# A one-core hybrid layer on TensorE: side transfers pinned behind their sources, weight loads ahead of their splits, the preparation of heads spread out, centring copies pinned on ScalarE

## The chip, the cores and the metric

One core of a Trainium2 chip runs the whole kernel. The metric is the device time of one execution in microseconds (us); lower is better. The engines are TensorE (PE, with its weight loads PEld), VectorE (DVE), ScalarE (ACT), GpSimd (POOL) and SyncE (SP), which issues the DMAs here. Each engine works through its own instructions in order.

## The reference

One layer on a sequence of 256 frames of width 4096, batch 1, in float32. One input projection feeds two groups of heads and a gate; their gated outputs go through an output projection and a LayerNorm.

```python
x <- LayerNorm(ALPHA * x + W_out(concat(fox, rwkv) * silu(z)))
# input projection: [fox q|k|v|f, rwkv r|k|v|w_down|a_down, gate z]
# fox:  16 heads of 128: logit[t,s] = q_t.k_s/sqrt(Dh) + sum_{s<j<=t} log f_j, softmax over s<=t, times v
# rwkv: 32 heads of 64: RWKV-7 time mixing in chunks of 64 frames, with a 2-tap shift of its inputs,
#       low-rank decay and in-context rate, per-head GroupNorm and a bonus term (r.k * r_k) * v
```

In a chunk the recurrence becomes a triangular system, which is solved row by row; between chunks a state is carried on with matmuls.

## The kernel before, in words

**Weights.** The two projections stream their weights as tiles of 512 KB. A tile `w{n}_{b}_{q}` belongs to group n (0 to 7), block b (0 to 3) and piece q (0 to 15) of the depth; the output projection's tiles are `wo{b}_{q}`. SP loads a tile (tag `wr`, four buffers), ACT casts it to a high half `...h` (L140, four buffers), DVE subtracts to get a low half `...l` (L141, three buffers), and PE does twelve 128x512 matmuls with it: x-high by w-high (L146), x-low by w-high (L147), x-high by w-low (L148). The two instructions of L140 and L141 are called the split of a tile here. In the profile the digits in names are left out, so `w_12l` stands for the low half of piece 12 of any group and block; the order rows keep the block and piece.

**Side work.** Everything else runs beside this stream, as Python generators in a list `sides`. After every six matmuls the kernel calls `slot()`, which advances each of them to its next `yield`; `wait(n)` yields n times. For each group n (four rwkv heads as two pairs i, two fox heads) these are:

- `prepare(i)`: token shift, low-rank decay and rates, the running sum of decays (L416), exponentials, the key's norm `np` by matmul (L467, L468), its reciprocal `n2` (L470, L472), and the factors `lt`, `BK` and `sb` (L448 to L476).
- `rwkv(n)`: products of chunks `gp` on PE (L491), masked on DVE to `gb` and `lt` (L508, L516), stored as `nd` and loaded back as `Nb` (L511, L512); then the triangular system, a chain of 31 pairs TENSOR_TENSOR (L535) and TENSOR_REDUCE (L538) on DVE; after it the centring: mean `vm` (L563), `SV` (L570) and its copies `UV` on ACT (L573); then inverses and state matmuls (L579 to L647).
- In the course of the chain v is transposed (L542), stored and loaded back in another order (`turn`, `vv`), and multiplied into the bonus (`bon`, L549). The constant `V_AT` says at which row.
- `fox(i)`: logits, exponentials and read-out of an attention head; `gate` multiplies the result by the gate and splits it into `hl`, which goes to DRAM (`hd`, L365).
- `unload`: copies a finished block from PSUM to `bk` (ACT), transposes it on DVE (L750), stores it (`bt`, in `turn`), and loads it back as `raw`, `fq`, `fk`, `zf`, `zr`.

**What sets the order.** A scheduler takes the program and puts each engine's instructions in an order by dependences and its own estimates; a tile's buffers come free when their last reader is done. `tc.keep_in_program_order(x)` pins x: on its engine it comes behind everything that was traced before it. The first pair of a chain is pinned so, and the v transposes.

The weights reach the stream through `fetch()`, which issues a tile's load and its split together, up to three tiles ahead of the matmuls. The functions as they were:

Of the kernel before, what the change touches and what calls it, by code (L numbers as in the profile page):

```python
# [17 lines left out]
P = 128  # L18
# [23 lines left out]
LAG = 2  # L42
LAND = 3
BEHIND = 13
V_AT = 6
W = {"fo": 3, "vs": 2, "np": 6, "gp": 5, "tp": 4, "d1": 8, "d2": 12, "xp": 3, "fs": 4, "fp": 5}
NB = D // OB
# [37 lines left out]
def layer(ctx: ExitStack, tc: tile.TileContext, xt, xtok, w_lora, w_main, muv, w_o, up, par, mulora, fbias, lng, lnb, cst, out):  # L85
# [124 lines left out]
    rpool = None  # L210
    ready = []

    def fetch():
        if stream:
            name, src = stream.pop()
            raw = wpool.tile([P, 1024], F32, tag="wr", name=name, bufs=4)
            nc.sync.dma_start(out=raw, in_=src.rearrange("p k c -> p (k c)"))
# [12 lines left out]
    def weights(name):  # L230
        while len(ready) < 3 and stream:
            fetch()
        got, hi, lo = ready.pop(0)
        assert got == name
        return hi, lo
# [35 lines left out]

    def turn(src, cols, name):
        d = dram.tile([cols // B, B, 2, 4, B], F32, tag=f"dt{cols}", name=name, bufs=2)
# [69 lines left out]

    kept_h = set()
    ht = {}
    closed = []
# [9 lines left out]
    def gate(y, key, k):  # L356
        far = k < FAR
        h = rp.tile([P, S], F32, tag="h", name=f"h{k}")
        nc.vector.scalar_tensor_tensor(h, y, 0.5, szs[key], ALU.mult, ALU.mult)
        pool, tag, bufs = (rp, "hl", 2) if far else (xpool, f"x{k}", 1)  # L360
        hl = pool.tile([P, 2, S], F32R, tag=tag, name=f"hl{k}", bufs=bufs)
        nc.scalar.copy(hl[:, 0, :], h)
        nc.vector.tensor_tensor(hl[:, 1, :], h, hl[:, 0, :].bitcast(F32), ALU.subtract)
        if far:
            nc.sync.dma_start(out=hd[k], in_=flat(hl).bitcast(F32))  # L365
            kept_h.add(k)
        else:
            ht[k] = hl
# [62 lines left out]
    def prepare(i):  # L431
# [30 lines left out]
        for j in range(2):  # L462
            h = HALF[j]
            nc.vector.tensor_tensor(BK[h, :, KB[j][1]], ch(k)[h], ch(eI)[h], ALU.mult)
# [6 lines left out]
        nc.scalar.copy(q["bon"][:, u, :], nps[:, S:])  # L471
        nc.vector.reciprocal(n2, n2)  # L472
        nc.vector.scalar_tensor_tensor(ae, ae, 0.5, n2, ALU.mult, ALU.mult)
        for j in range(2):
            h = HALF[j]
            nc.vector.scalar_tensor_tensor(BK[h, :, KB[j][0]], ch(kr)[h], column("k_k", i)[h], ch(ae)[h], ALU.mult, ALU.mult)  # L476
        prepared.add(i)

    def rwkv(n):
# [41 lines left out]
        for u in range(2):  # L521
# [3 lines left out]
            nc.scalar.copy(flat(BKt[:, u]), tp)  # L525
        yield from wait(W["d1"])
        prod = rp.tile([P, 2, NJ, B], F32, tag="prod", name=f"prod{n}")
        xc = rp.tile([P, 2, NJ, B], F32, tag="xc", name=f"xc{n}")
# [4 lines left out]
        for t, s in enumerate(range(B - 2, -1, -1)):  # L533
# [4 lines left out]
            nc.vector.tensor_reduce(xc[:, :, :, s : s + 1], prod[:, :, :, s:], AX.X, ALU.add)  # L538
            if t == V_AT:
                vst = UV[0].rearrange("p u c v -> p (u c v)").rearrange("p (m q) -> p m q", m=2)  # L540
                for a in range(2):
                    tc.keep_in_program_order(nc.vector.transpose(vst[:, a, :], vs_[n][:, a, :]))  # L542
            if t == V_AT + 2:
                vdr = turn(vst, 2 * P, f"vt{n}")
            if t == V_AT + 4:
                vv[n] = rp.tile([P, 2, S], F32, tag="s2", name=f"vv{n}")
                nc.sync.dma_start(out=vv[n], in_=turned_back(vdr))
            if t == V_AT + 8:
                nc.vector.tensor_tensor(flat(bon), flat(bon), flat(vv[n]), ALU.mult)  # L549
                for u in range(2):  # L550
                    nc.scalar.activation(bon[:, u], bon[:, u], AF.Identity, bias=column("gn_bias", i0 + u))
                bonned.add(n)
            if t % ROWS == ROWS - 1:
# [11 lines left out]
        for j in range(2):  # L565
            o = HALF[1 - j]
            for c in range(2):
                h = HALF[c]
                for a in range(2):
                    nc.vector.scalar_tensor_tensor(  # L570
                        SV[j][o, :, 2 * a + c, :], vm[h, a, :, j].unsqueeze(2).to_broadcast([C, 2, HD]), -1.0 / HD, vt[h, a, :, j, :], ALU.mult, ALU.add
                    )
            nc.scalar.copy(UV[j][o], SV[j][o])  # L573
            nc.gpsimd.memset(SV[j][HALF[j], :, 0, :], 0.0)
# [89 lines left out]
        for u in range(2):  # L664
# [4 lines left out]
            while f"r{i0 + u}" not in szs or 2 * (i0 + u) + 1 >= FAR and not closed:  # L669
                yield  # L670
            gate(yc[:, u], f"r{i0 + u}", 2 * (i0 + u) + 1)
        done.add(n)
# [3 lines left out]
    def fox(i, q, k, vt):  # L676
# [32 lines left out]
        while f"f{i}" not in szs or 2 * i >= FAR and not closed:  # L709
            yield  # L710
        gate(o, f"f{i}", 2 * i)
        foxed.add(i)
# [24 lines left out]
    def unload(n, b, bk, vt):  # L737
# [10 lines left out]
        if not last:  # L748
            for m in range(2):
                nc.vector.transpose(bk[:, m, :], bk[:, m, :])  # L750
            yield
            d = turn(bk, OB, f"bt{n}_{b}")
            unloading.clear()
            yield
        if b == 0:
            for u in range(2):
                i = 2 * n + u
                while n and n - 1 not in bonned:
                    yield
                raw = rp.tile([P, 2, S], F32, tag="s2", name=f"raw{i}")  # L760
                nc.sync.dma_start(out=raw, in_=turned_back(d[8 * u : 8 * u + 8]))
# [19 lines left out]
        else:  # L781
            for j, t in enumerate((fq, fk, zf, zr)):
                nc.sync.dma_start(out=t, in_=d[4 * j : 4 * j + 4].rearrange("b i m a t -> (b i) (m a t)"))
                if j % 2:
# [269 lines left out]
```

## Time and profile before

| | |
|---|---|
| median of 3 runs | 1972.52 us (1970.55 to 1972.55) |
| the profiled execution | 1970.62 us; span from first to last instruction 1968.8 us |
| granted TensorE clock, mean | 0.996 |
| busy: PE, PEld, DVE, ACT, POOL | 99%, 81%, 70%, 50%, 4% |
| instructions on PE, DVE, ACT, POOL | 10169, 2212, 1485, 111 |
| DMA | 420.14 MB, mean 213 GB/s |

A row of a timeline shows start and duration in us, the engine, the line and operation, what is written from what, shapes, how often, and in brackets the idle time of the engine ahead of it and what ended that. A row of the waits shows the waiting engine and line, the releaser, the sum in us, how often, and the longest. SPq is SP's DMA queue. The profiled execution lies at the low end of the three times.

### The profile page before, as it was taken

What the parts mean: (1) busy time and instruction counts of PE and PEld (TensorE: products, weight loads), DVE (VectorE), ACT (ScalarE), POOL (GpSimd) and SP (SyncE); (2) the same over time, 40 slices, a digit from 0 to 9 for tenths busy, and PEclk for the clock granted to TensorE, in tenths of its full rate; (3) what the DMA queues carried; (4) which work ended last, traced back from release to release, by engine and by line L of the source; (5) the groups of instructions that cost most, each with busy time, mean ns of one, the idle gap of its engine ahead of it and who ended that gap; (6) DMA issues with size and microseconds to landing.
All of it is one profiled execution on the core that took longest, in us unless ns stands there. A gap on an engine that the chain in (4) does not pass through costs nothing.

```text
span 1968.8 us, 28251 instructions
## 1 busy us (share of the span) xinstructions
PE 1942.4 (99%) x10169; PEld 1587.5 (81%) x10169; DVE 1370.1 (70%) x2212; ACT 983.3 (50%) x1485; POOL 75.1 (4%) x111
## 2 busy tenths in 40 slices
PE   9999999999999999999999999999999999999998
PEld 8877787878787878787878787878787878888886
DVE  6588568866785778577857785778577857755555
ACT  6554465456545654564456445644564454444332
POOL 0010001000100010001000100010001000000000
PEclk9999999999999999999999999999999999999999
DMA  9567666867676767676767676767677777766664
GB/s 336 149 212 217 193 208 193 241 185 221 200 231 191 220 201 224 192 220 206 226 184 230 199 227 186 228 205 225 187 219 215 242 269 250 242 198 199 195 194 169
DMA packets 269393, 420.14 MB, mean 213 GB/s; under 512 B 142338, under 2 KB 171028, under 8 KB 269252
## 3 DMA queue, kind: packets, MB, share of 16 engines
q1 hardware_dynamic: 268820, 417.91, 69.4%
q8 instruction: 80, 1.31, 0.3%
q14 instruction: 61, 0.50, 0.1%
q10 hardware_dynamic: 432, 0.43, 0.1%
HBM read 388.61 MB, written 29.64 MB: 212 GB/s over the span
## 4 chain that ended last, share of the span: by engine, by line
PE 94%; DVE 3%; ACT 1%; issue 1%; DMA 1%; POOL 0%; SPq 0%; POOLq 0%; DVEq 0%; ACTq 0%
PE acc L146 23%; PE acc L148 23%; PE acc L147 22%; PE oacc L821 6%; PE oacc L822 6%; PE oacc L823 6%; PE yp L647 1%; PE gp L491 1%; PE up L622 1%; PE rh L595 1%; PE sp L631 0%; DVE w_12l L141 0%; ACT w_14h L140 0%; PE fsp L686 0%; PE tp L524 0%
## 5 line engine op out<-in xcount | busy, mean ns | idle before, releaser
L538 DVE TENSOR_REDUCE xc<-prod 128x8 f32<-128x16 f32 (+30 forms) x248 | 73.1, 295 | 6.3
L535 DVE TENSOR_TENSOR prod<-Nb,xc 128x8 f32<-128x8 f32 (+30 forms) x248 | 71.8, 290 | 7.0 <-DMA Nb<-nd 0.3
L141 DVE TENSOR_TENSOR w_8l<-w,w_8h 128x1024 fp32r<-128x1024 f32 x31 | 38.0, 1225 | 52.5 <-PE acc L148 27.3
L140 ACT CAST w_7h<-w 128x1024 fp32r<-128x1024 f32 x31 | 32.6, 1051 | 57.4 <-DMA w<-in_w_main_dram 43.0
L141 DVE TENSOR_TENSOR w_5l<-w,w_5h 128x1024 fp32r<-128x1024 f32 x31 | 40.3, 1300 | 29.9 <-PE acc L148 10.8
L148 PE MATMUL acc<-w_12l,x 128*128 128x512 f32 x124 | 47.7, 402 | 10.7 <-DVE w_12l L141 10.7
L141 DVE TENSOR_TENSOR w_6l<-w,w_6h 128x1024 fp32r<-128x1024 f32 x31 | 37.8, 1219 | 28.0 <-ACT UV L625 15.8
L141 DVE TENSOR_TENSOR w_3l<-w,w_3h 128x1024 fp32r<-128x1024 f32 x31 | 37.9, 1222 | 27.2 <-PE acc L148 26.1
L140 ACT CAST w_15h<-w 128x1024 fp32r<-128x1024 f32 x31 | 32.7, 1054 | 48.1 <-DMA w<-in_w_main_dram 25.7
L140 ACT CAST w_8h<-w 128x1024 fp32r<-128x1024 f32 x31 | 32.6, 1050 | 47.8 <-PE acc L147 30.4
L146 PE MATMUL acc<-w_6h,x 128*128 128x512 f32 x124 | 49.7, 401 | 4.8 <-ACT w_6h L140 4.8
L141 DVE TENSOR_TENSOR w_7l<-w,w_7h 128x1024 fp32r<-128x1024 f32 x31 | 37.8, 1219 | 22.5 <-PE acc L148 10.9
L140 ACT CAST w_14h<-w 128x1024 fp32r<-128x1024 f32 x31 | 32.6, 1052 | 39.9 <-PE acc L147 16.9
L141 DVE TENSOR_TENSOR w_9l<-w,w_9h 128x1024 fp32r<-128x1024 f32 x31 | 37.9, 1223 | 20.8 <-PE acc L148 10.5
L141 DVE TENSOR_TENSOR w_4l<-w,w_4h 128x1024 fp32r<-128x1024 f32 x31 | 37.9, 1221 | 20.8 <-PE acc L148 20.8
L146 PE MATMUL acc<-w_5h,x 128*128 128x512 f32 x124 | 50.7, 409 | 0.0
L146 PE MATMUL acc<-w_0h,x 128*128 128x512 f32 x124 | 50.6, 408 | 0.0
L146 PE MATMUL acc<-w_1h,x 128*128 128x512 f32 x124 | 50.5, 408 | 0.0
L146 PE MATMUL acc<-w_3h,x 128*128 128x512 f32 x124 | 50.4, 406 | 0.0
L146 PE MATMUL acc<-w_4h,x 128*128 128x512 f32 x124 | 50.0, 403 | 0.0
L146 PE MATMUL acc<-w_2h,x 128*128 128x512 f32 x124 | 49.9, 402 | 0.0
L146 PE MATMUL acc<-w_13h,x 128*128 128x512 f32 x124 | 49.8, 401 | 0.0
(812 smaller groups left out, 6486.6 us busy)
## 6 DMA issues: line engine op xcount, KB each, us to landing
w<-in_w_main_dram SPq DMA_DIRECT2D x496, 512.0 KB
wo<-in_w_o_dram SPq DMA_DIRECT2D x128, 512.0 KB
bt<-bk SPq DMA_DIRECT2D x88, 128.0 KB
Nb<-nd SPq DMA_DIRECT2D x16, 512.0 KB
wr<-in_w_main_dram SPq DMA_DIRECT2D x15, 512.0 KB
hd<-hl SPq DMA_DIRECT2D x29, 256.0 KB
h<-hd SPq DMA_DIRECT2D x29, 256.0 KB
raw<-bt SPq DMA_DIRECT2D x16, 256.0 KB
```

Source lines behind the costliest of these rows:

```text
L140: nc.scalar.copy(hi[:, :n], src[:, :n])
L141: nc.vector.tensor_tensor(lo[:, :n], src[:, :n], hi[:, :n].bitcast(F32), ALU.subtract)
L146: nc.tensor.matmul(acc[:, :n], xs[k][:, 0, tt], hi[:, o : o + n], start=(k == 0), stop=False)
L147: nc.tensor.matmul(acc[:, :n], xs[k][:, 1, tt], hi[:, o : o + n], start=False, stop=False)
L148: nc.tensor.matmul(acc[:, :n], xs[k][:, 0, tt], lo[:, o : o + n], start=False, stop=(k == KT - 1))
L491: nc.tensor.matmul(gp[u][j][:, c * P : (c + 1) * P], BK[h, u, c, :], lt[j][h, u, c, :], start=True, stop=True)
L535: first = nc.vector.tensor_tensor(prod[:, :, :, s + 1 :], nb[:, :, s : s + 1, s + 1 :].to_broadcast([P, 2, NJ, w]), xc[:, :, :, s + 1 :], ...
L538: nc.vector.tensor_reduce(xc[:, :, :, s : s + 1], prod[:, :, :, s:], AX.X, ALU.add)
L595: nc.tensor.matmul(rh[HALF[j], u * C : (u + 1) * C], lt[j][:, u, c, 0:C], SV[j][:, u, c, :], start=True, stop=True)
L821: nc.tensor.matmul(acc, ht[k][:, 0, tt], hi, start=(k == 0), stop=False)
L822: nc.tensor.matmul(acc, ht[k][:, 1, tt], hi, start=False, stop=False)
L823: nc.tensor.matmul(acc, ht[k][:, 0, tt], lo, start=False, stop=(k == KT - 1))
```

## The change

Five things change; the computation does not.

1. `issue()` pins a DMA on SP's queue. The stores of `turn`, the loads of `raw`, `fq`, `fk`, `zf`, `zr`, `vv` and the stores `hd` use it. `turn` is now a generator that yields after every two stores (or every one); `gate` is a generator that waits three slots (`SENT`) before its store and holds while more than one is on its way; `unload` waits two slots ahead of `turn`.
2. `load()` issues weight tiles up to three ahead of their splits; `fetch()` takes them from `raws`. The buffers stay four.
3. `prepare` has more `yield`s; the reciprocal of `n2` is pinned and two slots pass after it. `W["np"]` goes from 6 to 4.
4. The transposes of v, `turn`, `vv` and `bon` become a generator `turns()` that advances by one step with each row of the chain.
5. The `UV` copies of the centring are pinned on ACT.

```diff
-V_AT = 6
-W = {"fo": 3, "vs": 2, "np": 6, "gp": 5, "tp": 4, "d1": 8, "d2": 12, "xp": 3, "fs": 4, "fp": 5}
+SENT = 3
+W = {"fo": 3, "vs": 2, "np": 4, "gp": 5, "tp": 4, "d1": 8, "d2": 12, "xp": 3, "fs": 4, "fp": 5}
...
-    def fetch():
+    raws = []
+
+    def load():
         if stream:
             name, src = stream.pop()
             raw = wpool.tile([P, 1024], F32, tag="wr", name=name, bufs=4)
             nc.sync.dma_start(out=raw, in_=src.rearrange("p k c -> p (k c)"))
+            raws.append((name, raw))
+
+    def fetch():
+        while len(raws) < 3 and stream:
+            load()
+        if raws:
+            name, raw = raws.pop(0)
...
-    def turn(src, cols, name):
+    def issue(out, src):
+        tc.keep_in_program_order(nc.sync.dma_start(out=out, in_=src))
+
+    def turn(src, name, each=2):
...
         for a in range(4):
-            nc.sync.dma_start(out=d[:, :, :, a, :].rearrange("q i m t -> i m q t"), in_=s[B * a : B * (a + 1)])
+            issue(d[:, :, :, a, :].rearrange("q i m t -> i m q t"), s[B * a : B * (a + 1)])
+            if a % each == each - 1:
+                yield
         return d
...
     def gate(y, key, k):
         far = k < FAR
+        while len(storing) > 1:
+            yield
...
         if far:
-            nc.sync.dma_start(out=hd[k], in_=flat(hl).bitcast(F32))
+            storing.append(k)
+            yield from wait(SENT)
+            issue(hd[k], flat(hl).bitcast(F32))
             kept_h.add(k)
+            storing.remove(k)
...
         nc.vector.scalar_tensor_tensor(sb[:, 1, :], r, column("r_k", i), k, ALU.mult, ALU.mult)
+        yield
...
         nc.vector.tensor_tensor(sl, flat(sb), sh.bitcast(F32), ALU.subtract)
+        yield
...
         nc.scalar.copy(lt[1][HALF[1]], lt[0][HALF[1]])
+        yield
...
         nc.scalar.copy(q["bon"][:, u, :], nps[:, S:])
-        nc.vector.reciprocal(n2, n2)
+        yield
+        tc.keep_in_program_order(nc.vector.reciprocal(n2, n2))
+        yield from wait(2)
...
+        def turns():
+            yield from wait(4)
...
+                tc.keep_in_program_order(nc.vector.transpose(vst[:, a, :], vs_[n][:, a, :]))
+            yield from wait(3)
+            d = yield from turn(vst, f"vt{n}", 1)
+            yield from wait(2)
...
+            issue(vv[n], turned_back(d))
+            yield from wait(4)
+            nc.vector.tensor_tensor(flat(bon), flat(bon), flat(vv[n]), ALU.mult)
...
+        other = turns()
...
-            if t == V_AT:
...
-            if t == V_AT + 2:
...
-            if t == V_AT + 4:
...
-            if t == V_AT + 8:
...
+            next(other, None)
...
-            nc.scalar.copy(UV[j][o], SV[j][o])
+            tc.keep_in_program_order(nc.scalar.copy(UV[j][o], SV[j][o]))
...
-            yield
-            d = turn(bk, OB, f"bt{n}_{b}")
+            yield from wait(2)
+            d = yield from turn(bk, f"bt{n}_{b}")
```

What this does to the order, at three places. The first is DVE in group 1, block 1, between the splits of pieces 11 and 12, where the second head of a pair is prepared; names with `_2` and `_3` ahead of the number belong to heads 2 and 3 of the list. Before:

```order
L141 TENSOR_TENSOR w_1_11l<-w_1_11_3000,w_1_11h 128x1024
L472 RECIPROCAL n_2926<-n_2926 128x256
L414 TENSOR_SCALAR tw_2952<-tw_2952 128x256
L473 SCALAR_TENSOR_TENSOR ae_2681<-ae_2681,n_2926 128x256
L416 SCALAR_TENSOR_TENSOR L_2969<-cs,tw_2952 128x256
L476 SCALAR_TENSOR_TENSOR BK_2845<-s_2_2827,prm,ae_2681 64x4x64 x2
L448 TENSOR_TENSOR k_2986<-s_3_2884,am_2982 128x256
L426 SCALAR_TENSOR_TENSOR ae_2984<-ta_2954,eI_2974 128x256
L451 SCALAR_TENSOR_TENSOR sb_2988<-s_3_2881,prm,k_2986 128x256
```

After:

```order
L141 TENSOR_TENSOR w_1_11l<-w_1_11_2913,w_1_11h 128x1024
L493 TENSOR_SCALAR n_2966<-np_2963 128x256
L141 TENSOR_TENSOR w_1_12l<-w_1_12_2933,w_1_12h 128x1024
L496 RECIPROCAL n_2966<-n_2966 128x256
L141 TENSOR_TENSOR w_1_13l<-w_1_13_2951,w_1_13h 128x1024
L498 SCALAR_TENSOR_TENSOR ae_2793<-ae_2793,n_2966 128x256
L141 TENSOR_TENSOR w_1_14l<-w_1_14_2976,w_1_14h 128x1024
L501 SCALAR_TENSOR_TENSOR BK_2873<-s_2_2861,prm,ae_2793 64x4x64 x2
```

Before, thirteen instructions (these and `lt`, `lt` and `BK` twice) stood ahead of the split of piece 12; now one does, and the others stand between later splits. It is the same in the groups after it.

The second is DVE in group 0, block 3, at the end of the chain. Before:

```order
L538 TENSOR_REDUCE xc_1610<-prod_1609 128x8
L535 TENSOR_TENSOR prod_1609<-Nb_1465,xc_1610 128x8x31
L538 TENSOR_REDUCE xc_1610<-prod_1609 128x8
L563 TENSOR_REDUCE vm_2034<-vs_1339 128x8
L570 SCALAR_TENSOR_TENSOR SV_0_1484<-vm_2034,vs_1339 64x2x64 x4
L570 SCALAR_TENSOR_TENSOR SV_0_1485<-vm_2034,vs_1339 64x2x64 x4
L141 TENSOR_TENSOR w_3_6l<-w_3_6_1855,w_3_6h 128x1024
L141 TENSOR_TENSOR w_3_7l<-w_3_7_1893,w_3_7h 128x1024
```

After:

```order
L582 TENSOR_REDUCE xc_1692<-prod_1691 128x8
L579 TENSOR_TENSOR prod_1691<-Nb_1547,xc_1692 128x8x31
L582 TENSOR_REDUCE xc_1692<-prod_1691 128x8
L141 TENSOR_TENSOR w_3_7l<-w_3_7_1804,w_3_7h 128x1024
L722 SCALAR_TENSOR_TENSOR lg_1962<-fsp_1959,ct,nb_1903 128x128
```

The chain begins behind w_3_0l now (before: behind w_2_12l) and ends ahead of w_3_7l, with 27 of its instructions in one piece behind w_3_6l; `vm` and `SV` stand ahead of the split of `w_0_1` of the next group. In groups 1 to 6 the chain begins behind w_2_12l instead of w_2_10l, and ends ahead of w_3_7l in both.

The third is ACT at the same place. Before:

```order
L140 CAST w_3_5h<-w_3_5_1833 128x1024
L573 COPY UV_0_1486<-SV_0_1484 64x512
L573 COPY UV_0_1487<-SV_0_1485 64x512
L140 CAST w_3_6h<-w_3_6_1855 128x1024
L140 CAST w_3_7h<-w_3_7_1893 128x1024
```

After:

```order
L140 CAST w_0_1h<-w_0_1_2086 128x1024
L140 CAST w_0_2h<-w_0_2_2109 128x1024
L604 COPY UV_0_1568<-SV_0_1566 64x512
L604 COPY UV_0_1569<-SV_0_1567 64x512
L890 COPY bk_3_2171<-acc_3_0_1724 128x512
L890 COPY bk_3_2171<-acc_3_1_1725 128x512
L140 CAST w_0_3h<-w_0_3_2153 128x1024
```

The copies have moved from between the casts of block 3, pieces 5 and 6, to behind the cast of piece 2 of the next group's first block.

More of the change, by code (lines that the diff above doesn't have):

```diff
@@ L230, in weights @@
     def weights(name):
-        while len(ready) < 3 and stream:
+        while len(ready) < 3 and (stream or raws):
             fetch()
@@ L344, in layer @@
     kept_h = set()
+    storing = []
     ht = {}
@@ L476, in prepare @@
             nc.vector.scalar_tensor_tensor(BK[h, :, KB[j][0]], ch(kr)[h], column("k_k", i)[h], ch(ae)[h], ALU.mult, ALU.mult)
+        yield
         prepared.add(i)
@@ L670, in rwkv @@
                 yield
-            gate(yc[:, u], f"r{i0 + u}", 2 * (i0 + u) + 1)
+            yield from gate(yc[:, u], f"r{i0 + u}", 2 * (i0 + u) + 1)
         done.add(n)
@@ L710, in fox @@
             yield
-        gate(o, f"f{i}", 2 * i)
+        yield from gate(o, f"f{i}", 2 * i)
         foxed.add(i)
@@ L760, in unload @@
                 raw = rp.tile([P, 2, S], F32, tag="s2", name=f"raw{i}")
-                nc.sync.dma_start(out=raw, in_=turned_back(d[8 * u : 8 * u + 8]))
+                issue(raw, turned_back(d[8 * u : 8 * u + 8]))
                 yield from wait(LAND)
@@ L782, in unload @@
             for j, t in enumerate((fq, fk, zf, zr)):
-                nc.sync.dma_start(out=t, in_=d[4 * j : 4 * j + 4].rearrange("b i m a t -> (b i) (m a t)"))
+                issue(t, d[4 * j : 4 * j + 4].rearrange("b i m a t -> (b i) (m a t)"))
                 if j % 2:
```

19 lines of the change are left out of this document (8 added, 11 removed).

## The prediction

> **What bounds the kernel now.** I read the page first, then the waits of the matmul engine, then windows around the longest of them, then the timelines of the engines that end those waits.
>
> ```profile
> PE 1942.4 (99%) x10169; PEld 1587.5 (81%) x10169; DVE 1370.1 (70%) x2212; ACT 983.3 (50%) x1485; POOL 75.1 (4%) x111
> PE 94%; DVE 3%; ACT 1%; issue 1%; DMA 1%; POOL 0%; SPq 0%; POOLq 0%; DVEq 0%; ACTq 0%
> ```
>
> PE is busy in 99% of a span of 1968.8 us and has 94% of the chain that ended last. The matmuls themselves don't change, so the change can only win what PE loses: 1968.8 − 1942.4 = 26.4 us, and a little more where the clock falls. PE's waits say where that is:
>
> ```profile
> PE acc L148 <- DVE w_12l L141: 10.7, 7, 1.5
> PE acc L146 <- ACT w_6h L140: 4.8, 1, 4.8
> PE gp L491 <- DVE BK L476: 0.5, 1, 0.5
> PE acc L148 <- DVE w_14l L141: 0.2, 1, 0.2
> ```
>
> Two things carry it: seven equal waits for the low half of a weight tile 12, 1.5 us each, and one wait of 4.8 us for the high half of a tile 6. The other idle time lies in startup and tail, which the change doesn't reorder. The windows show what these waits cost with the clock:
>
> ```profile
> 185.00:190.00 5.00, 0.19 (x2) 0.09 (x1) 3.24 (x12) 2.31 (x4) 0.00 (x0) 0.94 0.03 11
> 190.00:195.00 5.00, 4.96 (x11) 3.47 (x12) 4.01 (x5) 3.74 (x6) 0.00 (x0) 0.50 0.54 140
> 195.00:200.00 5.00, 5.00 (x22) 4.15 (x22) 3.21 (x8) 2.77 (x6) 0.00 (x0) 0.88 0.66 210
> 500.00:520.00 20.00, 18.48 (x84) 15.03 (x83) 18.33 (x27) 10.55 (x18) 0.41 (x2) 1.00 0.53 163
> ```
>
> Columns: window, length, PE, PEld, DVE, ACT and POOL busy with counts, granted clock, DMA. A short wait (500:520) leaves the clock at 1.00. After the long one the clock is 0.50 for 5 us, in which PE does 11 matmuls, and 0.88 for the next 5.
>
> **The seven short waits, and what they are worth.** One of them, on DVE and then on PE:
>
> ```profile
> 501.44 1.22 DVE L141 TENSOR_TENSOR w_11l<-w,w_11h 128x1024 fp32r<-128x1024 f32 x1
> 502.57 1.75 DVE L472 RECIPROCAL n<-n 128x256 f32<-128x256 f32 x1
> ...
> 508.63 0.85 DVE L464 TENSOR_TENSOR BK<-k,eI 64x256 f32<-64x256 f32 x2
> 509.51 1.23 DVE L141 TENSOR_TENSOR w_12l<-w,w_12h 128x1024 fp32r<-128x1024 f32 x1
> 508.88 0.39 PE L147 MATMUL acc<-w_12h,x 128*128 128x512 f32 x1
> 510.79 0.74 PE L148 MATMUL acc<-w_12l,x 128*128 128x512 f32 x2 [1.52 <-DVE w_12l L141]
> 511.37 0.40 PE L146 MATMUL acc<-w_12h,x 128*128 128x512 f32 x1
> ```
>
> Between the splits of tiles 11 and 12 DVE does 6.9 us (502.57 to 509.51) of the preparation of a head, and PE stands at 510.79. The spread of prepare breaks exactly this piece: in the new order one short instruction (n2 from np) stands between those splits, and the rest comes one or two at a time, at most four, behind tiles 12 to 17. The sum np that this instruction reads is at the same place on PE as before. So no tile here has more than about 2.5 us of other work between it and the next, against 6.9. I count the seven waits as gone. Their worth: 10.7 us as idle rows; by starts, 510.79 − 508.88 = 1.91 instead of the usual 0.23, and 0.58 instead of 0.45 for the next two, so 1.81 each and 12.7 in seven. I take 12.0, between the two. The pinned reciprocal with its wait costs nothing here: behind it on DVE stands only a split that already has its data.
>
> **The one long wait in the first group.**
>
> ```profile
> 153.85 0.17 DVE L535 TENSOR_TENSOR prod<-Nb,xc 128x8 f32<-128x8 f32 x1
> 155.71 1.22 DVE L141 TENSOR_TENSOR w_13l<-w,w_13h 128x1024 fp32r<-128x1024 f32 x1
> 156.85 0.20 DVE L538 TENSOR_REDUCE xc<-prod 128x8 f32<-128x48 f32 x1
> ...
> 178.53 1.22 DVE L141 TENSOR_TENSOR w_5l<-w,w_5h 128x1024 fp32r<-128x1024 f32 x1
> 185.54 0.68 DVE L563 TENSOR_REDUCE vm<-vs 128x8 f32<-128x512 f32 x1
> 186.25 2.02 DVE L570 SCALAR_TENSOR_TENSOR SV<-vm,vs 64x128 f32<-64x128 f32 x8
> 189.90 1.23 DVE L141 TENSOR_TENSOR w_6l<-w,w_6h 128x1024 fp32r<-128x1024 f32 x1 [1.63 <-ACT w_6h L140]
> 187.28 0.61 ACT L573 COPY UV<-SV 64x512 f32<-64x512 f32 x1 [11.87 <-DVE SV L570]
> 183.81 0.39 PE L147 MATMUL acc<-w_5h,x 128*128 128x512 f32 x1
> 184.72 0.39 PE L148 MATMUL acc<-w_5l,x 128*128 128x512 f32 x1
> 189.92 0.80 PE L146 MATMUL acc<-w_6h,x 128*128 128x512 f32 x1 [4.81 <-ACT w_6h L140]
> ```
>
> ACT held the UV copies ahead of the cast of tile 6 and waited in them for DVE, which was ending the chain of 31 pairs. Pinning the copies on ACT takes them behind w1_0_2h, out of this place. But the reason behind it, the chain on DVE, stays. In the new order the whole chain of the first group stands between the splits of w0_3_0 and w0_3_7, with 27 chain instructions in one piece ahead of w0_3_7l. The sum: four matmuls start in 184.72 − 183.81 = 0.91 us, so a tile of 12 takes PE 2.73. A split occupies DVE 1.14 (155.71 to 156.85). The chain with its transposes ran from 153.85 to 185.54 = 31.7 with nine splits in it (9 × 1.14 = 10.3) and 0.6 for bon, which now comes later: 20.8 of its own. New: split 0 (1.14), chain 20.8, six splits (6.84), split 7 (1.22), together 30.0 us after the start S of split 0. PE's need is bounded by the buffers of low halves:
>
> ```profile
> 543.84 1.23 DVE L141 TENSOR_TENSOR w_9l<-w,w_9h 128x1024 fp32r<-128x1024 f32 x1 [1.50 <-PE acc L148]
> 549.48 0.39 PE L148 MATMUL acc<-w_9l,x 128*128 128x512 f32 x1
> ```
>
> With three buffers a split waits for PE, and is then read 549.48 − 543.84 = 5.64 after it begins. So w0_3_7l is needed at S + 5.64 + 7 × 2.73 = S + 24.7, and PE waits 5.3 us there, against 189.92 − 184.72 − 0.23 = 4.97 now. I enter +0.4. Bounds: −5 if the chain gets its DVE time earlier than I think, +1.5 if Nb or a transpose comes late.
>
> The clock adds to it: 190:195 held 11 matmuls where 22 fit (2.5 us), and 12% of 195:200 is 0.6. That the short waits cost nothing of this kind and the long one 3.1 us, the rows show; where between 1.5 and 4.8 us the clock begins to fall they don't. The wait I expect, 5.3, lies beyond the one that has the drop, so the sum keeps the clock's cost unchanged. The Trainium skill, TensorE: Matmul & The Clock Gate, Part 1: The HAM clock gate, puts it at an idle window of about 3.4 us that runs freely. By that rule a wait of 5.3 us keeps the penalty, which is the sum as I make it, and one cut below about 3.4 us would lose the whole 3.1; the trace agrees with both sides of it as far as it goes (1.5 us: 1.00; 4.8 us: 0.50).
>
> The two smaller rows (gp behind BK 0.5, w_14l 0.2) belong to preparation in this group that is now spread: −0.7.
>
> **What is late next.** In the other groups the chain moves two tiles later (from behind w2_2_10l to behind w2_2_12l) and must still end ahead of w2_3_7l:
>
> ```profile
> 547.71 0.17 DVE L535 TENSOR_TENSOR prod<-Nb,xc 128x8 f32<-128x8 f32 x1
> ...
> 582.15 1.22 DVE L141 TENSOR_TENSOR w_7l<-w,w_7h 128x1024 fp32r<-128x1024 f32 x1
> ```
>
> From 547.71 to 582.15 are 34.4 us with twelve splits, so 20.8 without them. New: 1.14 + 20.8 + ten splits (11.4) + 1.22 = 34.6 from the start of split 12; needed at 5.64 + 11 × 2.73 = 35.7. A margin of 1.1 us, in six groups, if split 12 and its successors have their weights in time. They may not, since the block-matrix Nb lands among them:
>
> ```profile
> 343.22 0.36 SPq L217 DMA_DIRECT2D w<-in_w_main_dram  x1
> 349.94 1.05 ACT L140 CAST w_10h<-w 128x1024 fp32r<-128x1024 f32 x1 [3.91 <-DMA w<-in_w_main_dram]
> 352.60 0.18 DVE L535 TENSOR_TENSOR prod<-Nb,xc 128x8 f32<-128x8 f32 x1 [0.34 <-DMA Nb<-nd]
> ```
>
> A weight tile queued between the two halves of Nb landed 6.7 us after its issue, and the chain waited for Nb. A lateness of that kind up to 3 us is a stall up to 1.9 a group, 11 in six. The lower end is 0, where the margin holds. I take +1.5, near the lower end, since five splits lie between the last long DVE piece (gb) and the chain, in which DVE gets ahead again; it also has to pay for small waits in the reshuffled attention steps around w_3_10.
>
> **Pinned side transfers and weights ahead of splits.** No engine issues more or fewer instructions than before; these edits change when, and what SP's queue holds back.
>
> ```profile
> SPq L365 <- DVE hl L363: 81.2, 22, 7.1
> ACT w_7h L140 <- DMA w<-in_w_main_dram: 43.0, 12, 4.7
> ```
>
> Now a store of hl at the head of SP's queue holds the weight loads behind it for up to 7.1 us, and ACT waits for weights, 12 times up to 4.7 us. With three loads in front and the stores sent three slots later both should fall. But none of the ACT waits is in PE's list, so the gain is 0: splits lie some 4 us ahead of PE and hide it. The bounds: no gain, since PE lost nothing; a loss where a pinned store waits for its source with loads behind it, priced by the same 7.1 us less the loads now ahead (three tiles, 8.2 us): nothing. The vt transposes as a generator give vv later by some slots; it is read by bon alone, which now stands behind w_3_8l, before anything reads it: 0. The gate's generator, which holds a second store back, delays h by a few slots; h is read back in the output projection, long after: 0. Steps on PE that move with the spread (lp, np and gp of the second head, two tiles later) are the same matmuls in the same stream: 0, as long as what they read is ready, and it is since they follow their sources.
>
> **Sum.** 1970.62 (profiled run; span 1968.8) − 12.0 − 0.7 + 0.4 + 1.5 = 1959.8. The median shown is 1972.52, 1.9 above the profiled run, so 1961.7; I say 1961.5.
>
> **Rivals.** (1) The forecast: short waits gone, the long one moved to w0_3_7l with its clock cost, stalls at w_3_7l small. (2) The long wait goes too, since the chain of the first group needs less DVE time than I summed or splits have more lead: another −5 to −8.1 with the clock, 1953 to 1956; a wait left but too short for the clock, 1958.5. For it: nothing else than DVE holds tile 7. Against it: 5.3 us is more than any error I see in rows of 0.2 to 0.4 us. (3) The short waits return at w_3_7l: the margin of 1.1 us is smaller than the lateness of weights beside Nb, and six waits of 1.0 to 1.7 us come back, 1966 to 1971. For it: the landing of 6.7 us; against it: the chain starts two tiles later than Nb does now. (4) Slower, by one mechanism: weight loads on SP's queue behind pinned side transfers arrive late at the beginning of the chain in all groups. Each group would have to lose 12.3 / 7 = 1.8 us to be even, and 2.4 to be 0.2% slower (1976.5), that is, weights 2.9 to 3.5 us later at w_2_13 than worked out. At 4 us late it is 1980. Against it: three loads are ahead.
>
> **Chances.** Forecast 0.60, (2) 0.15, (3) 0.20, (4) 0.05. About 0.2%, 3.9 us, is what a measurement of this kernel can tell from no change. Faster is below 1968.6: (1), (2) and half of (3), less a little, 0.83; same 0.12; slower 0.05. The range goes from the far end of (2), 1953, to the middle of (3), 1968.5.
>
> **What would show it.** Right: no row of PE waiting for w_12l; windows 300:320 and so on at 20.00; a wait of some 5 us for w_7l around the chain's end in the first group, with a clock of 0.50 behind it; waits for w_7l in later groups below 1 us. Wrong: no long wait at all with the clock at 1.00 (rival 2), six or seven rows of w_7l above 1 us (rival 3), or ACT waiting for weights with PE behind it (rival 4).

## The result, and the profile after

The changed kernel takes 1959.32 us (median of 4 runs, 1957.89 to 1961.03) against 1971.68 for the kernel before in the same runs: a ratio of 0.9938, 95% interval 0.9921 to 0.9955. The profiled execution has a span of 1956.1 us, 12.7 less than the 1968.8 of before. The forecast was 1961.5 us, and 1959.8 for the profiled execution, which took 1957.89. Time and waits came out near it; why the short waits went, the experiments below show, and it is not quite what the prediction said.

The page of the changed kernel, busy times, and then the longest of its waits on PE between startup and tail:

```profile
PE 1937.4 (99%) x10169; PEld 1586.9 (81%) x10169; DVE 1368.3 (70%) x2212; ACT 981.2 (50%) x1485; POOL 81.2 (4%) x111
```

```profile
PE acc L148 <- DVE w_7l L141: 5.4, 1, 5.4
PE xp L637 <- DVE Q L620: 1.1, 1, 1.1
PE acc L148 <- DVE w_8l L141: 1.0, 1, 1.0
```

The row of w_12l with its seven waits is gone, and so are gp behind BK and w_14l. The long wait has moved from the cast of tile 6 to the low half of tile 7, 5.4 us instead of 4.8. Two short ones are new: w_8l behind it, and xp behind Q, once. The windows around the long wait, and the one that held a w_12l wait before:

```profile
185.00:190.00 5.00, 1.91 (x9) 1.25 (x7) 4.59 (x13) 1.53 (x3) 0.00 (x0) 1.00 0.42 163
190.00:195.00 5.00, 2.73 (x7) 2.15 (x7) 2.15 (x4) 0.00 (x0) 0.00 (x0) 0.71 0.32 101
195.00:200.00 5.00, 3.96 (x18) 2.99 (x17) 2.97 (x7) 0.72 (x3) 0.00 (x0) 0.95 0.03 8
500.00:520.00 20.00, 20.00 (x92) 16.61 (x92) 16.73 (x24) 12.30 (x23) 0.84 (x3) 1.00 0.68 207
```

The clock (third column from the end) falls again behind the long wait, for a shorter time than before. The timeline of DVE and PE there:

```profile
186.52 0.39 PE L147 MATMUL acc<-w_7h,x 128*128 128x512 f32 x1
190.67 0.42 DVE L582 TENSOR_REDUCE xc<-prod 128x8 f32<-128x256 f32 x1
191.01 1.21 DVE L141 TENSOR_TENSOR w_7l<-w,w_7h 128x1024 fp32r<-128x1024 f32 x1
192.27 0.79 PE L148 MATMUL acc<-w_7l,x 128*128 128x512 f32 x1 [5.37 <-DVE w_7l L141]
197.03 0.74 DVE L722 SCALAR_TENSOR_TENSOR lg<-fsp,ct,nb 128x128 f32<-128x128 f32 x2 [4.81 <-PE fsp L717]
197.69 1.22 DVE L141 TENSOR_TENSOR w_8l<-w,w_8h 128x1024 fp32r<-128x1024 f32 x1
```

The chain ends at 191.0 and only then DVE splits tile 7. The last two rows show the new small wait: lg stands ahead of the split of tile 8 on DVE, waits 4.8 us for fsp on PE, and so makes w_8l late. In the groups after it the margin at this place holds; group 2:

```profile
581.46 1.22 DVE L141 TENSOR_TENSOR w_7l<-w,w_7h 128x1024 fp32r<-128x1024 f32 x1
583.11 0.39 PE L148 MATMUL acc<-w_7l,x 128*128 128x512 f32 x1
```

The split ends at 582.68, PE reads it at 583.11: 0.43 us to spare, where the sum gave 1.1.

### The profile page after: what moved, and what is told of

Its sections match the earlier page's. It is cut to its first block, busy times and chain, and to the rows that moved or that the text cites. A ratio compares the mean times of both kernels' runs of the same rounds, so it can differ in the third digit from the quotient of the medians.

```text
span 1956.1 us, 28202 instructions
## 1 busy us (share of the span) xinstructions
PE 1937.4 (99%) x10169; PEld 1586.9 (81%) x10169; DVE 1368.3 (70%) x2212; ACT 981.2 (50%) x1485; POOL 81.2 (4%) x111
## 4 chain that ended last, share of the span: by engine, by line
PE 86%; DMA 1%; DVE 0%; ACT 0%; issue 0%; DVEq 0%; ACTq 0%; SPq 0%
PE acc L146 21%; PE acc L148 20%; PE acc L147 20%; PE oacc L852 6%; PE oacc L854 6%; PE oacc L853 6%; PE yp L678 1%; PE gp L517 1%; PE up L653 1%; PE rh L626 1%; PE sp L662 0%; DMA wo<-in_w_o_dram 0%; PE fsp L717 0%; PE fop L736 0%; PE tp L550 0%; DMA h<-hd 0%
## 5 line engine op out<-in xcount | busy, mean ns | idle before, releaser
L141 DVE TENSOR_TENSOR w_10l<-w,w_10h 128x1024 fp32r<-128x1024 f32 x31 | 37.9, 1223 | 37.8 <-PE acc L148 21.6
L141 DVE TENSOR_TENSOR w_8l<-w,w_8h 128x1024 fp32r<-128x1024 f32 x31 | 37.8, 1219 | 32.9 <-ACT UV L656 13.6
L141 DVE TENSOR_TENSOR w_0l<-w,w_0h 128x1024 fp32r<-128x1024 f32 x31 | 37.9, 1222 | 31.3 <-ACT w_0h L140 14.8
L148 PE MATMUL acc<-w_7l,x 128*128 128x512 f32 x124 | 49.5, 399 | 5.4 <-DVE w_7l L141 5.4
L141 DVE TENSOR_TENSOR w_11l<-w,w_11h 128x1024 fp32r<-128x1024 f32 x31 | 37.9, 1222 | 21.0 <-PE acc L148 13.5
L141 DVE TENSOR_TENSOR w_12l<-w,w_12h 128x1024 fp32r<-128x1024 f32 x31 | 37.5, 1211 | 20.6 <-PE acc L148 16.1
L141 DVE TENSOR_TENSOR w_14l<-w,w_14h 128x1024 fp32r<-128x1024 f32 x31 | 38.0, 1227 | 19.9 <-issue 11.1
L140 ACT CAST w_0h<-w 128x1024 fp32r<-128x1024 f32 x31 | 32.7, 1053 | 38.3 <-PE acc L147 21.7
L140 ACT CAST w_5h<-w 128x1024 fp32r<-128x1024 f32 x31 | 32.6, 1053 | 37.9 <-PE acc L147 37.9
L146 PE MATMUL acc<-w_7h,x 128*128 128x512 f32 x124 | 51.0, 411 | 0.0
L146 PE MATMUL acc<-w_8h,x 128*128 128x512 f32 x124 | 50.0, 404 | 0.4 <-ACT w_8h L140 0.4
L140 ACT CAST w_9h<-w 128x1024 fp32r<-128x1024 f32 x31 | 32.4, 1046 | 35.6 <-PE acc L147 32.9
```

The lines of the kernel that those rows point to most:

```text
L140: nc.scalar.copy(hi[:, :n], src[:, :n])
L141: nc.vector.tensor_tensor(lo[:, :n], src[:, :n], hi[:, :n].bitcast(F32), ALU.subtract)
L146: nc.tensor.matmul(acc[:, :n], xs[k][:, 0, tt], hi[:, o : o + n], start=(k == 0), stop=False)
L148: nc.tensor.matmul(acc[:, :n], xs[k][:, 0, tt], lo[:, o : o + n], start=False, stop=(k == KT - 1))
```

## The experiments

Each experiment below is timed against the kernel before on the same chip (1970.6 to 1971.1 us in these comparisons). The changed kernel's 1959.3 is from its own comparison. The waits and timelines are those of one profiled execution of each kernel.

**Without the spread.** The edit, on the changed kernel:

```diff
-W = {"fo": 3, "vs": 2, "np": 4, "gp": 5, "tp": 4, "d1": 8, "d2": 12, "xp": 3, "fs": 4, "fp": 5}
+W = {"fo": 3, "vs": 2, "np": 6, "gp": 5, "tp": 4, "d1": 8, "d2": 12, "xp": 3, "fs": 4, "fp": 5}
...
-        yield
-        tc.keep_in_program_order(nc.vector.reciprocal(n2, n2))
-        yield from wait(2)
+        nc.vector.reciprocal(n2, n2)
```

and the four other added yields of prepare taken out.

> The changed kernel with prepare as it was before (no added yields, reciprocal of n2 not pinned, np wait 6). Theory A, that spreading prepare is what took away the seven waits: they come back, and the time is 1959 + 12.7 = 1972 us. Theory B, from the order of this kernel: the split of w_1_12 now stands in the middle of the second head's preparation, behind 6 of its instructions instead of 13 (about 3.8 us instead of 6.9), so its wait is gone without the spread, and w_1_13l is at a margin of about 0 (a wait of 0 to 0.5 us in seven groups); and in the first group the chain begins behind w0_2_13l, which gives 1.14 + 20.3 + 9 x 1.14 + 1.22 = 33.0 us up to w0_3_7l against a need of 5.64 + 10 x 2.73 = 32.9, so that the wait of 5.4 us there and its clock go as well: 1951 to 1956 us, faster than the changed kernel.

Measured: 1953.01 us, ratio 0.9909 (0.9892 to 0.9925), faster than the change as a whole. PE's waits:

```profile
PE acc L148 <- DVE w_11l L141: 1.4, 6, 0.2
PE acc L148 <- DVE w_7l L141: 0.8, 1, 0.8
```

Theory A falls. The seven waits are gone without the spread, and so is the long one: 33.0 against 32.9 was the sum at w0_3_7l, 0.8 is the wait. The timeline of DVE in group 2, where 6.9 us stood in one piece before:

```profile
492.87 1.75 DVE L492 RECIPROCAL n<-n 128x256 f32<-128x256 f32 x1
...
495.60 0.96 DVE L496 SCALAR_TENSOR_TENSOR BK<-s,prm,ae 64x256 f32<-64x256 f32 x2
496.59 1.22 DVE L141 TENSOR_TENSOR w_12l<-w,w_12h 128x1024 fp32r<-128x1024 f32 x1
497.73 0.53 DVE L446 SCALAR_TENSOR_TENSOR ae<-ta,eI 128x256 f32<-128x256 f32 x1
...
499.75 0.85 DVE L484 TENSOR_TENSOR BK<-k,eI 64x256 f32<-64x256 f32 x2
500.63 1.22 DVE L141 TENSOR_TENSOR w_13l<-w,w_13h 128x1024 fp32r<-128x1024 f32 x1
```

The split of tile 12 stands in the middle: 3.7 us ahead of it, 2.9 behind. Nothing in prepare was changed here. Something else in the edit has moved it against the weight stream.

**The spread alone**, the reverse of that edit on the kernel before.

> The kernel before with the spread of prepare alone. If the spread is all that matters: about 1959 us. From the order of this kernel: the waits for w_12l go (-13), but 43 DVE instructions in one piece (chain, vm and SV) now stand ahead of w0_3_5l: from the start of w0_2_15l 1.14 + 20.3 + 2.7 + 5 x 1.14 + 1.22 = 31.1 us and the UV copy ahead of the cast, against a need of 5.64 + 6 x 2.73 = 22.0, a wait of 9 to 10 us and some 3 us of slow clock in the first group instead of 8 in all, +4 to +6; and w_3_7l of the other groups is at a margin of about 0 with vm and SV ahead of it, 0 to 1 us six times. In all 1963 to 1969 us.

Measured: 1976.95 us, ratio 1.0029 (1.0019 to 1.0039): slower than before. Waits, and windows of the first group:

```profile
PE acc L146 <- ACT w_5h L140: 10.4, 1, 10.4
PE acc L146 <- ACT w_7h L140: 8.0, 6, 1.6
```

```profile
185.00:190.00 5.00, 0.00 (x0) 0.00 (x0) 4.72 (x11) 0.00 (x0) 0.00 (x0) 0.76 0.23 93
190.00:195.00 5.00, 2.06 (x4) 1.24 (x5) 3.70 (x12) 4.22 (x9) 0.00 (x0) 0.50 0.00 0
195.00:200.00 5.00, 5.00 (x17) 3.93 (x17) 3.94 (x4) 3.78 (x4) 0.00 (x0) 0.72 0.72 205
```

The w_12l waits are gone here too, and the wait of 10.4 us in the first group is near the one summed (9 to 10). The time missed its range by 8 us. One part is the size of the other wait: six waits for w_7h of 8.0 us in all where 0 to 6 was summed. Another was not foreseen: at the end of the last group PE waits twice for xp (0.9 and 1.1 us), and the clock falls behind it (see the last section). The first of the w_7h waits, on ACT:

```profile
393.77 0.62 ACT L579 COPY UV<-SV 64x512 f32<-64x512 f32 x1 [8.95 <-DVE SV L576]
394.79 0.62 ACT L579 COPY UV<-SV 64x512 f32<-64x512 f32 x1 [0.40 <-DVE SV L576]
395.32 1.04 ACT L140 CAST w_7h<-w 128x1024 fp32r<-128x1024 f32 x1
```

Unpinned UV copies stand ahead of the cast of tile 7 and hold it behind the chain and the centring in every group. I had counted the centring on DVE but not the copy, the cast and the subtraction that then follow one another.

**The UV pin alone**, on the kernel before.

```diff
-            nc.scalar.copy(UV[j][o], SV[j][o])
+            tc.keep_in_program_order(nc.scalar.copy(UV[j][o], SV[j][o]))
```

> The kernel before with the UV copies pinned on ACT alone. If the copies on ACT are what made the long wait: it goes with its clock, -8 us, 1963. If it is the chain on DVE: the order on DVE is unchanged, w_6l can be split at 188.3 instead of 189.9 and PE does the high half's first matmuls meanwhile, so the wait moves to w_6l and shrinks by about 1 us, with the clock as before: 1970 to 1971 us.

Measured: 1969.86 us, ratio 0.9996 (0.9986 to 1.0005), no change. PE waits for `w_6l` 5.8 us instead of `w_6h` 4.8: the cast now runs at 181.8, early enough, and the wait stands on DVE's chain as before. It didn't shrink by 1 us as I expected, since the chain itself ended 1.4 us later in this execution (186.9 against 185.5). So the copy on ACT was the last link, and the chain on DVE the cause.

**The rows of the first chain pinned**, on the changed kernel.

```diff
-            if not t:
+            if not t or not n:
                 tc.keep_in_program_order(first)
```

> The changed kernel with the first instruction of every row of the chain pinned in the first group, so that it spreads over w0_3_0 to w1_0_0 and no piece of 27 stands ahead of w0_3_7l. Theory: the wait of 5.4 us, the slow clock behind it (1.6) and the waits for w_8l (1.2) go, -8 us: 1951 us, with the clock at 1.00 all through. Rival: the piece of 18 instructions (9 of the chain, vm, SV; 6.5 us) that then stands ahead of w1_0_1l makes a new wait of up to 2 us: 1953. Were it not the chain on DVE that held w0_3_7l, the time would stay at 1959.

Measured: 1952.90 us, ratio 0.9906 (0.9891 to 0.9921).

```profile
PE acc L148 <- DVE w_8l L141: 1.0, 1, 1.0
PE acc L148 <- DVE w_1l L141: 0.8, 1, 0.8
PE xp L637 <- DVE Q L620: 0.5, 1, 0.5
```

The wait of 5.4 us is gone but for 0.4, and its slow clock is gone too (mean granted clock 0.999 against 0.998 for the change), which shows that the one piece of 27 chain instructions made it. The rival's new wait is there as well (w_1l, 0.8), and w_8l stayed.

**Neither spread nor delayed unload**, on the changed kernel: as in the first experiment, and besides

```diff
-            yield from wait(2)
-            d = yield from turn(bk, f"bt{n}_{b}")
+            yield
+            d = yield from turn(bk, f"bt{n}_{b}", 9)
```

with which turn issues its four stores in one step.

> The changed kernel with prepare as before, as in the first experiment, and with unload as before too: one yield ahead of turn, and its four stores in one step, so that raw, and with it the preparation, comes three slots earlier. The pins on SP and ACT, the loads ahead and the generator of the v transposes stay. Theory (what broke up the preparation in the first experiment is this delay of three slots): 13 instructions stand in one piece again ahead of w_1_11l or w_1_12l, the seven waits of 1.5 us are back, and in the first group the chain begins behind w0_2_12l again with a piece of 23 ahead of w0_3_6l and a wait of 5 to 6 us: 1969 to 1971 us. Rival (the pins and the loads ahead matter by themselves): it stays at about 1953.

Measured: 1978.66 us, ratio 1.0038 (1.0024 to 1.0051).

```profile
PE acc L148 <- DVE w_12l L141: 10.1, 6, 1.8
PE acc L146 <- ACT w_13h L140: 3.9, 6, 1.0
PE acc L148 <- DVE w_6l L141: 3.6, 1, 3.6
PE acc L148 <- DVE w_11l L141: 1.4, 1, 1.4
ACT w_13h L140 <- DMA w<-in_w_main_dram: 32.3, 6, 6.8
SPq L281 <- DVE post L693: 49.3, 6, 8.7
```

The seven waits are back (six of w_12l, one of w_11l), 11.5 us. So what broke up the preparation in the first experiment was the later unload. The time itself I missed by 8 us: a wait for w_13h came six times that nobody expected, and the waits for w_12l are longer, 1.8 against 1.5. These two rows give 3.9 + 0.8 us. The wait in the first group is 3.6 and not 5 to 6, so that sum was off too. What made w_13h late, the last two rows show: ACT waits for its weights, and SP's queue stands still ahead of a pinned transfer (the row names post, from which h and hl are made). In group 2 SP issues the four stores of bt together, then nothing from 448.8 to 456.0, when hl is ready and its pinned store hd goes out; the next weight load leaves behind it at 456.4, and ACT casts tile 13 only at 461.4. This is the mechanism of the prediction's rival (4), at another place (block 0) and in a kernel that issues its stores in one step. No run of this kernel without the pins was made, so the pins' part in it is read from these rows alone.

**One number in the kernel before.** No edit of the change is in this one.

```diff
-            yield
+            yield from wait(4)
             d = turn(bk, OB, f"bt{n}_{b}")
```

> The kernel before with one number changed: unload waits four slots instead of one ahead of turn; none of the five edits is in it. Theory: the delay alone moves the preparation by three slots, the split of w_1_12 falls into the middle of it, and the chain of the first group begins one tile later (behind w0_2_13l, to w0_3_6l): 1.14 + 20.3 + 8 x 1.14 + 1.22 = 31.8 us against a need of 5.64 + 9 x 2.73 = 30.2, a wait of 1.6 us without slow clock instead of 8 in all. Seven waits of 1.8 go, w_11l may wait 0.4 six times as in the first experiment: 1954 to 1958 us. Rival (the pins and the loads ahead are needed): 1968 or more.

Measured: 1960.99 us, ratio 0.9949 (0.9934 to 0.9964). One number gives 9.8 of the change's 12.4 us.

```profile
PE acc L148 <- DVE w_6l L141: 2.7, 1, 2.7
PE acc L148 <- DVE w_11l L141: 1.3, 6, 0.2
```

```profile
185.00:190.00 5.00, 2.80 (x7) 2.22 (x8) 3.97 (x7) 1.35 (x3) 0.00 (x0) 0.65 0.34 94
190.00:195.00 5.00, 5.00 (x17) 3.91 (x16) 2.45 (x2) 1.99 (x3) 0.00 (x0) 0.66 0.75 232
```

The w_12l waits are gone, as the theory had it. It came out 3 us above its range, because the wait in the first group was 2.7 instead of 1.6 and, unlike what I wrote, slowed the clock: 0.65 and 0.66 in the ten us from 185.

**The same with five slots** (`wait(5)`).

> The same with five slots instead of four. If it were later arrival as such that helps, it would help as much: 1954 to 1958 us. If it is where the pieces happen to fall between the splits: at five slots the order has 14 instructions of the preparation in one piece again (ahead of w_1_13l, 1.1 to 1.5 us of wait seven times), and 33 instructions (chain, vm, SV) ahead of w0_3_6l, a wait of 6 to 7 us with its clock: 1969 to 1974 us.

Measured: 1970.49 us, ratio 1.0004 (0.9994 to 1.0013), no change to before.

```profile
PE acc L146 <- ACT w_6h L140: 8.1, 1, 8.1
PE acc L148 <- DVE w_13l L141: 1.8, 7, 0.3
PE acc L148 <- DVE w_11l L141: 1.7, 6, 0.3
```

One slot more gives back all of the gain. The 33 instructions ahead of w0_3_6l cost 8.1 us where 6 to 7 was summed (the profiled execution, at 1973.96 us, is 3.5 above the median); the piece of 14 now ahead of w_13l costs only 0.3 each and not 1.1 to 1.5, a part of the sum that was too high and wasn't pursued. Later as such is not better: what counts is where the pieces fall between the splits.

**No pins on SP**, on the changed kernel.

```diff
     def issue(out, src):
-        tc.keep_in_program_order(nc.sync.dma_start(out=out, in_=src))
+        nc.sync.dma_start(out=out, in_=src)
```

> The changed kernel with the side transfers not pinned on SP. The order on DVE around the chain and the preparation is the same as in the changed kernel (27 chain instructions ahead of w0_3_7l, 9 ahead of w_3_7l). If the pins matter only by SP's queue, which PE doesn't feel: 1958 to 1961 us, the same wait of some 5 us for w0_3_7l. If they keep weights from being late: slower by more than 2 us, with ACT's waits for weights in PE's list.

Measured: 1956.69 us, ratio 0.9929 (0.9913 to 0.9946), within the interval of the changed kernel's 0.9938. PE still waits 4.9 us for w_7l. That is 1.3 us below the range of the first case and nowhere near the second: the pins win nothing that can be measured in this kernel. Its runs are all faster than those of the changed kernel (1956.20 to 1957.73 against 1957.89 to 1961.03), but from another comparison, and the intervals of the ratios overlap; that the pins cost something is not shown.

**No loads ahead**, on the changed kernel.

```diff
     def fetch():
-        while len(raws) < 3 and stream:
-            load()
+        load()
```

> The changed kernel with a weight tile's load emitted together with its split again. The prediction put the loads ahead at 0. From the order of this kernel they count, by where the splits are placed: 32 chain instructions then stand ahead of w0_3_6l (1.14 + 20.9 + 5 x 1.14 + 1.22 = 29.0 us against 5.64 + 6 x 2.73 = 22.0, a wait of 7 us in place of 5.4), and in groups 1 to 6 the chain must end ahead of w_3_6l (1.14 + 20.8 + 9 x 1.14 + 1.22 = 33.4 against 32.9, and the margin came out 0.7 below the sum there, so a wait of about 1.2 us six times): 1964 to 1969 us. If the order didn't matter: 1959.

Measured: 1965.44 us, ratio 0.9974 (0.9965 to 0.9984).

```profile
PE acc L148 <- DVE w_6l L141: 12.8, 7, 7.1
```

One wait of 7.1 us in the first group (7 summed), and six of 5.7 us in all, 0.95 each (1.2 summed). So the loads ahead are worth some 6 us, and by the order on DVE: with them the split of one more tile stands ahead of the chain's end, which delays w_7l and not w_6l.

**Towards a faster version.** First the kernel without the spread, with its two last waits taken on:

```diff
-            if not t:
+            if not t or not n and t > 24:
                 tc.keep_in_program_order(first)
...
+                    if j and not a and not c:
+                        tc.keep_in_program_order(centre)
...
             nc.gpsimd.memset(SV[j][HALF[j], :, 0, :], 0.0)
-        yield from wait(W["d2"] - 1)
+            yield
+        yield from wait(W["d2"] - 3)
```

where `centre` is the SV instruction.

> The first experiment's kernel (the change without the spread of prepare) with its two remaining waits taken away: a yield between the two halves of the centring, the second half pinned on DVE, so that w_3_11l has four SV instructions less ahead of it; and the last six rows of the first group's chain pinned, so that they come behind w0_3_7l. Theory: 6 x 0.4 and 1.0 us go, 1949.6 us. Rival: the moved instructions make w_3_12l or w0_3_14l late instead, 1951 to 1953.

Measured: 1951.27 us, ratio 0.9899 (0.9882 to 0.9915). Both rows are gone from PE's waits; of the 3.4 us hoped for, 1.7 are seen. Between startup and tail the profiled execution has three waits that are new or longer: w_8h 0.9 (0.4 without this edit) and bk 0.4 (0.2) in the first 100 us, and np 0.5, once in a later group. They are 1.2 us of what is missing; w_8h varies between 0.4 and 1.0 from kernel to kernel, so the edit need not have made that one longer. The rival's late tiles w_3_12l and w0_3_14l did not come.

Then the two orders together:

```diff
-        yield
+        if i > 1:
+            yield
...
-        yield from wait(W["np"] if n else 2 * W["np"])
+        yield from wait(W["np"] if n else 12)
```

for each yield of the spread in prepare and the pinned reciprocal (i counts the pairs of all groups, so both pairs of the first group stay as before), with the pins on the chain as above and `wait(2)` between the halves of the centring (so `W["d2"] - 5` behind them).

> The best of both: the changed kernel with prepare spread only from the second pair on (the first pair as before), the last six rows of the first group's chain pinned as in the fastest kernel so far, and the centring split in two. In the first group the order is then that of the fastest kernel (chain from behind w0_2_13l, no wait), in the others that of the changed one (no waits, 2.0 us gained a group against 1.4 there). Theory: 1949 to 1951 us, no wait of PE above 0.5 us between the startup and the tail. Rival: with the waits gone nothing more is to be had, 1951.3 as the fastest.

Measured: 1948.52 us (1947.72 to 1950.80), ratio 0.9890 (0.9876 to 0.9905), the fastest of all.

```profile
PE fpt L741 <- DVE lg L737: 0.9, 2, 0.6
PE xp L648 <- DVE Q L631: 0.8, 1, 0.8
PE acc L146 <- ACT w_8h L140: 0.6, 1, 0.6
```

Against 1959.3 it is 10.8 us better, most of it the first group's waits with their clock. Three small waits between startup and tail are still above the theory's 0.5 (0.6, 0.8 and 0.6).

## Why the prediction was right, and where it was not

**The seven short waits (−12.0).** They went. Their worth was a little more: the first matmul of w_4 in block 2 starts 4.45 us earlier than before in group 1 (338.64, now 334.19) and 16.46 earlier in group 7 (1512.48, now 1496.02), 12.0 in six groups and 2.0 each, against the 1.8 of the starts and the 1.5 of the idle rows. (Only the difference of the two counts: side matmuls that stand elsewhere in the new order shift each of these starts by some us.) So idle rows undercount these waits: the start-to-start reading was nearer.

**The reason given for it failed.** "The spread of prepare breaks exactly this piece" is true of the order, and enough by itself (the spread alone has no w_12l row). But the spread isn't needed: without it the waits are gone as well, since unload's longer way delays the preparation by three slots and the split falls into its middle. With both undone the waits come back. Two causes each do it. Both are in the diff; I had looked at one. And the spread's own price, a chain that begins later, outweighs what it adds: 1976.95 alone, and 1953.0 when it is left out of the change.

**The long wait (+0.4).** This sum was right to 0.2 us (5.3 foreseen; 5.53 measured by starts, which is how it was set against the 4.97 of before, and 5.37 as an idle row), from durations of the kernel before and the new order alone. The clock's part was not: I kept 3.1 us, and by the starts of matmuls it was about 1.6 (0.36 for the pair behind the gap and six steps of 0.2). That it fell is luck of this execution and not the change's doing: the kernel without pins on SP, with the same piece of 27 and a gap of 5.07 us, has 6.83 us of slow clock instead of 3.41 and loses about 2.7. The clock changes on steps of 3.41 us (last section), and a gap of 5.3 us is not sure to hold a whole one, so "keeps the penalty" did not follow. The sum also lacks another term, of which the rows show the cause: the wait for w_8l (1.0), made by lg, which is queued ahead of a split on DVE and waits for fsp on PE.

**w_3_7l (+1.5).** No wait there. The margin was 0.43 and not 1.1, but it held in all six groups. Weights beside Nb still come late for ACT (in group 2 the casts of tiles 12 and 13 wait 2.3 and 2.1 us for them), but not for DVE, whose split of tile 12 there waits for PE; that this is owed to the later start of the chain was not tested.

**Pins on SP and loads ahead (0).** For the pins nothing measurable came, as forecast. The reason given holds for the order of this kernel: PE has no wait for a cast above 0.4 us. With the stores bunched (neither spread nor delayed unload) a stuck queue did reach PE. Wrong for the loads: I looked for what they do to the transfers, found that nothing on PE waits for those, and entered 0. They count by the order in which the splits stand on DVE, about 6 us. The generator of the v transposes and the later stores of hl, also entered at 0, were not undone by themselves.

**The rest.** gp behind BK and w_14l went (−0.7), and xp behind Q (1.1) is new. With 14.0 for the seven waits, 0.7 for the small rows, −0.6 − 1.2 + 1.5 in the first group (longer gap, w_8l by starts, less slow clock) and −1.1 for xp the spans should differ by 13.3; they differ by 12.7. Rivals 2 to 4 didn't come about. Against the forecast of 1959.8 for this execution the seven waits, w_3_7l and the clock came out 2.0, 1.5 and 1.5 us better, the long gap, w_8l and xp 0.2, 1.2 and 1.1 worse: 7.5 us of errors, of which 1.9 are left in the total. That so much of them cancels is luck.

## What to carry to other kernels

Where a scheduler merges side work into a stream, ask of each edit what it does to the order at every narrow place, not only at the one it names: a delay of three slots elsewhere did as much as the edit that was made for the purpose, and a fourth took it back. A sum over one in-order queue (work between two splits, against tiles times the stream's period plus the lead that the buffers allow) gave most such waits to within 1 us, from measured durations and the new order alone; three it missed by 1.1 to 1.4 us. And undo the parts of a good change one by one: this one was better without its most plausible part.

## What the hardware showed

All gaps here go by the starts of matmuls, less one usual step. The granted clock falls already behind a gap of 2.85 us (the kernel with one number changed; clock 0.65 and 0.66 in two windows of 5 us, and 14 matmuls with 0.2 to 0.36 us added, 3.0 us in all), and not behind gaps of 1.97 us (w_12l in the kernel without spread and delay, clock 1.00 in the window 500:520). Nor does it take one long gap: in the kernel with the spread alone two of 1.1 us, one right behind the other (xp, up to 1599.9), were enough. The Trainium skill, TensorE: Matmul & The Clock Gate, Part 1: The HAM clock gate, gives an idle window of about 3.4 us; here 2.85 was enough.

What the clock goes by can be seen from when it changes. In each of the thirteen kernels it stays at 1.00 or 0.50 for whole multiples of 3.41 us, from its first rise up to its last change: in the kernel before for 54 of them at 1.00 (5.06 to 189.38), then two at 0.50 (to 196.21); in the changed kernel for one at 0.50, in the one with `wait(5)` for three. Windows laid on these steps, two of the kernel with one number changed, two of the spread alone, one of the changed kernel, and one of that without pins on SP:

```profile
183.12:186.53 3.41, 1.39 (x7) 0.81 (x5) 3.20 (x8) 0.00 (x0) 0.00 (x0) 1.00 0.10 40
186.53:193.36 6.83, 6.16 (x15) 4.80 (x16) 4.96 (x6) 3.34 (x4) 0.00 (x0) 0.50 0.60 179
1597.30:1600.71 3.41, 1.41 (x38) 0.86 (x39) 3.27 (x7) 2.16 (x4) 0.00 (x0) 1.00 1.02 396
1600.71:1604.12 3.41, 3.41 (x16) 2.72 (x15) 2.38 (x4) 1.27 (x2) 0.00 (x0) 0.50 1.04 393
192.12:195.53 3.41, 3.26 (x8) 2.58 (x9) 0.10 (x1) 0.00 (x0) 0.00 (x0) 0.50 0.49 154
191.69:198.52 6.83, 5.95 (x15) 4.80 (x16) 1.68 (x5) 0.00 (x0) 0.00 (x0) 0.50 0.26 77
```

So a step in which PE was busy for 1.4 of 3.41 us was followed by half the clock, without being idle throughout; one of 1.62 (the changed kernel, 185.29:188.71) was not. In the tail it followed steps of 1.74 and 1.75 as well (the kernel before, 1957.48:1960.90; the fastest, 1936.71:1940.12), so the border near half a step is not sharp here; the ends of matmuls are modelled. The loss doesn't grow with the gap: about 3 us behind 2.85 and 4.97 us, 2.7 behind 5.07, 1.6 behind 5.53, each in one execution. The same section of the Trainium skill has that window run freely, which makes both depend on where a gap falls in it; the traces agree, as the clock changes on steps of 3.41 us and not at a fixed time behind the start of a gap.
